# Reciprocal square roots as one power on GpSimd, weight splits on VectorE, last squares straight into the column sums

## The chip, the cores and the metric

The kernel runs on one core of one Trainium2 chip. The metric is the device time of one execution in microseconds (us), as the median of several runs. In the profile PE is TensorE (PEld its weight loads), DVE is VectorE, ACT is ScalarE, POOL is GpSimd and SP is SyncE, whose queue here issues the weight transfers. An L with a number is a line of the kernel; the changed kernel has fewer lines, so its numbers are a little smaller for the same statement.

## The reference

A sequence `x` of 256 tokens with 1024 features, and a context `ctx` of the same size, pass through two blocks in float32. The first block has two layers, each with a modulated feed-forward part, a convolution (layer 0) or windowed attention (layer 1), and a second feed-forward part; a norm with a learned gain closes it. The second block has two layers: a mixer (two kinds of block attention in layer 0, a compressed, a selected and a windowed attention in layer 1), a feed-forward part, and a gated embedding. What matters here is that a root mean square norm stands before every part, and over every head of 64 features of the second block's queries and keys:

```python
def rmsnorm(x, g):
    y = x * lax.rsqrt(jnp.mean(x * x, axis=-1, keepdims=True) + NORM_EPS)
    return y * g

def modulate(x, g, shift, scale):
    return rmsnorm(x, g) * (1 + scale) + shift

def swiglu(h, w_in, w_out):
    gate, up = jnp.split(h @ w_in, 2, axis=-1)
    return (jax.nn.silu(gate) * up) @ w_out

def first_block(...):
    for i in range(DEPTH):
        x = x + 0.5 * gt1 * swiglu(modulate(x, g1, sh1, sc1), ffn1_wi[i], ffn1_wo[i])
        ctx = ctx + 0.5 * cg1 * swiglu(modulate(ctx, g1, ch1, cs1), ffn1_wi[i], ffn1_wo[i])
        ...                              # convolution or attention on both, gated
        x = x + 0.5 * gt3 * swiglu(modulate(x, g3, sh3, sc3), ffn2_wi[i], ffn2_wo[i])
    return rmsnorm(x, final_g)

def second_block(...):
    for i in range(DEPTH):
        h = h + mixer(rms(h, norm_mix[i]))          # rms over each head of q and k inside
        h = h + swiglu(rms(h, norm_ffn[i]), ...)
        h = h + sigmoid(rms(h, norm_ple[i]) @ w_ple_gate[i]) * (p[i] @ w_ple_proj[i])
    return h
```

## The kernel before

Activations lie with features on the 128 partitions, in 8 chunks of 128 features by 256 tokens; the two sequences of the first block are called streams (0 is `x`, 1 is `ctx`). Every product of float32 matrices is made of three matmuls of a high and a low part (`mm3`, L337 to L339, and `mm_tm`, L360 to L362, for results with tokens on the partitions): high by high, high by low, low by high. So each weight tile that a DMA brings into a staging buffer `stg` is split: ACT copies it rounded into `wh` (L306), and a subtract makes `wl` (L308). That subtract runs on DVE, except that the first `on_pool[0]` of a tile's four or so pieces go to POOL. The number is `ABP` = 4, so all pieces, while the tiles of the first mixer of the second block are prepared, `NSP` = 2 for the second mixer, and 0 elsewhere; four pieces at the opening also go to POOL.

A norm works like this. As each chunk of the residual is finished (L657 in the feed-forward parts), `sq_add` squares it on ACT (L385) and POOL adds the square to an accumulator (L386). `rcol` sums over the features: `colsum` multiplies the accumulator with a column of ones on PE (L390), and DVE reads the result and adds epsilon (L397). `rsqrt_small` makes the reciprocal root with ten DVE instructions on 1 to 8 columns: a first guess by integer arithmetic (L370), then three Newton steps of three instructions (L373, L374, L376). `spread` turns the column into a row on all partitions: DVE scales the identity matrix with it (L406) and PE multiplies with ones (L407). In the first block `Mod.chunk` then modulates a chunk: DVE L543; for even chunks ACT L548 and DVE L549 give the high and low parts, for odd chunks ACT L551 and L552 and POOL L553 do. PE's first matmuls of the next part need these chunks, so each such seam of the first block is a chain from the last residual through PE, DVE and PE back to PE. In the second block, and for its first norm, `Norm` and `FinalNorm` let the matmuls start on unscaled activations and apply the root to their results. `FinalNorm.root` (L1373 to L1383) makes two roots one after the other, for the first block's closing norm and the second block's first; ACT's evictions of the projections (L1449) scale with the product of both.

In the mixers `qk_heads` calls `head_rms` for four heads on two token tiles: ACT squares (L1419), DVE scales epsilon (L1422), sums per head (L1423), takes the mean (L1425, two instructions), makes the root of 8 columns and applies it (L1437, two instructions); later PE transposes the result (L1463) and DVE moves it on (L1465). POOL also scales the rows of attention weights (L1485, L1486).

The program is emitted by loops over parts, layers and output tiles, with a small list of due times (`Flow`) that places side work between groups of matmuls; a scheduler of the framework then orders each engine's instructions. Engines run in that order and wait for each other by semaphores, so an instruction that waits holds up all that stands behind it on its engine. `look` asks for weights a tile or more ahead of their use. In the last rows below `L492` is DVE's sum that forms the modulation vectors.

## Time and profile before

| | |
|---|---|
| median of 3 runs | 2514.32 us (2513.06 to 2517.64) |
| the profiled execution | 2520.06 us, of which the trace spans 2518.2 |
| PE busy | 2360.3 us (94%) |
| DVE busy | 1754.9 us (70%), 3816 instructions |
| ACT busy | 1075.2 us (43%) |
| POOL busy | 569.3 us (23%), 595 instructions |
| the chain that ended last | PE 32%, DVE 9%, ACT 1% of the span (the page follows only a part of it) |
| granted clock of TensorE, mean | 0.97 |

A row of a timeline gives the start, the duration, the engine, the line and operation, the tiles written and read with their sizes, and how many instructions were put together; in brackets stands the idle time before it and what released it. A group of instructions gives the busy time of all, the mean of one, and the idle time before them with its releasers. A waiting PE counts twice: the pause itself, and the part of the work behind it at half clock, which the column of the granted clock shows (1.00 is 2.4 GHz, 0.5 is 1.2 GHz).

### The profile page before, as it was taken

To read this page: it belongs to the slowest core of one execution; us is meant where nothing else is said; L and a number is where in the kernel's file an instruction comes from. 1 tells how busy PE (TensorE), PEld (TensorE's weight loads), DVE (VectorE), ACT (ScalarE), POOL (GpSimd) and SP (SyncE) were. 2 spreads that over 40 slices of the span, in tenths; PEclk is the share of its full clock that TensorE was granted. 3 is DMA by queue.
4 is the path that set the end of the run, shared out by engine and by line. 5 is a ranking of instruction groups with operands and counts; after the bars stand their busy time and mean duration, and the time that the engine had idled before them with its cause. 6 is when DMAs were issued, how large, how long until landed. Compare 5 with 4: busy or idle time off the path is not lost. (4 is left out here: it accounts for less than half of the span.)

```text
span 2518.2 us, 40157 instructions
## 1 busy us (share of the span) xinstructions
PE 2360.3 (94%) x15397; PEld 2107.0 (84%) x15397; DVE 1754.9 (70%) x3816; ACT 1075.2 (43%) x2497; POOL 569.3 (23%) x595
## 2 busy tenths in 40 slices
PE   7999998766999999899999899999799999899999
PEld 5788887655888888888888888999699998879999
DVE  5567569887665745766546786767977678787667
ACT  3322223432532222332232485546455555665444
POOL 1100103665410010310010332104641112431101
PEclk9999998887999999999999999999899999999999
DMA  9745354152244535244546323865335556325553
GB/s 262 232 158 176 125 176 151 59 126 67 64 138 138 177 104 167 97 138 150 184 150 209 105 68 110 254 205 168 114 103 176 187 177 177 118 66 161 176 176 114
DMA packets 313149, 371.91 MB, mean 148 GB/s; under 512 B 9307, under 2 KB 298236, under 8 KB 305148
## 3 DMA queue, kind: packets, MB, share of 16 engines
q1 hardware_dynamic: 312380, 368.87, 46.1%
q8 instruction: 121, 1.98, 0.3%
q14 instruction: 72, 0.59, 0.1%
q10 hardware_dynamic: 576, 0.47, 0.1%
HBM read 364.06 MB, written 5.24 MB: 147 GB/s over the span
## 5 line engine op out<-in xcount | busy, mean ns | idle before, releaser
L337 PE MATMUL ps<-a,wh 128*128 128x256 f32 (+2 forms) x4032 | 1310.7, 327 | 20.3 <-ACT wh L306 9.2
L339 PE MATMUL ps<-a,wl 128*128 128x256 f32 (+2 forms) x4032 | 1310.0, 325 | 6.5 <-DVE wl L308 6.5
L338 PE MATMUL ps<-a,wh 128*128 128x256 f32 (+2 forms) x4032 | 1311.7, 326 | 3.7 <-DVE a L1290 1.4
L306 ACT ACTIVATE wh<-stg 128x512 fp32r<-128x512 f32 (+1 forms) x1280 | 609.5, 539 | 598.9 <-PE ps L338 328.5
L337 PEld LDWEIGHTS ps<-a,wh 128*128 128x128 f32 x4032 | 771.3, 192 | 93.1 <-ACT wh L306 11.2
L339 PEld LDWEIGHTS ps<-a,wl 128*128 128x128 f32 x4032 | 774.5, 192 | 68.0 <-DVE wl L308 7.5
L338 PEld LDWEIGHTS ps<-a,wh 128*128 128x128 f32 x4032 | 775.5, 192 | 66.6 <-POOL a L553 2.0
L308 DVE TENSOR_TENSOR wl<-stg,wh 128x512 fp32r<-128x512 f32 (+1 forms) x1206 | 692.7, 626 | 162.9 <-ACT wh L306 157.2
L561 POOL TENSOR_TENSOR a<-t,a 128x256 fp32r<-128x256 f32 (+1 forms) x128 | 136.2, 1066 | 1338.5 <-ACT a L560 1286.5
L492 DVE CUSTOM_DVE_ANT_0 void<-stg,cb,vec 128x1024 f32<-128x1024 f32 x208 | 276.7, 1330 | 41.3 <-DMA stg<-ada_t 37.4
L560 ACT ACTIVATE a<-t 128x256 fp32r<-128x256 f32 (+1 forms) x152 | 76.5, 504 | 254.9 <-DVE t L621 176.3
L657 DVE SCALAR_TENSOR_TENSOR a<-ps,mv,a 128x256 f32<-128x256 f32 x232 | 101.4, 477 | 77.2 <-PE ps L339 77.1
L621 DVE TENSOR_TENSOR t<-t,ps 128x512 f32<-128x512 f32 x66 | 45.4, 687 | 151.6 <-PE ps L339 139.1
L386 POOL TENSOR_TENSOR acc<-acc,t 128x256 f32<-128x256 f32 x98 | 95.7, 977 | 205.0 <-ACT t L385 201.8
L361 PE MATMUL ps<-wl,a 128*128 128x256 f32 x384 | 112.2, 292 | 8.2 <-DVE wl L308 6.9
L360 PE MATMUL ps<-wh,a 128*128 128x256 f32 x384 | 112.7, 294 | 1.7 <-ACT wh L306 1.7
L308 POOL TENSOR_TENSOR wl<-stg,wh 128x512 fp32r<-128x512 f32 (+1 forms) x74 | 93.8, 1296 | 88.7 <-ACT wh L306 88.7
L362 PE MATMUL ps<-wh,a 128*128 128x256 f32 x384 | 111.3, 290 | 0.0
L620 ACT ACTIVATE t<-ps 128x512 f32<-128x512 f32 x66 | 39.0, 590 | 108.2 <-PE ps L339 108.2
L361 PEld LDWEIGHTS ps<-wl,a 128*128 128x128 f32 x384 | 76.7, 200 | 9.7 <-DVE wl L308 7.3
L360 PEld LDWEIGHTS ps<-wh,a 128*128 128x128 f32 x384 | 76.5, 199 | 2.7 <-ACT wh L306 1.9
L841 DVE SCALAR_TENSOR_TENSOR a<-a,vec,a 128x512 f32<-128x512 f32 x76 | 78.3, 1095 | 0.0
(310 smaller groups left out, 1957.0 us busy)
## 6 DMA issues: line engine op xcount, KB each, us to landing
stg<-ffn_wi SPq DMA_DIRECT2D x86, 1024.0 KB, 5.1
stg<-ada_t SPq DMA_DIRECT2D x60, 1024.0 KB, 4.8
stg<-ffn_wo SPq DMA_DIRECT2D x48, 768.0 KB, 4.5
stg<-w_ffn_gate SPq DMA_DIRECT2D x22, 1024.0 KB, 5.4
stg<-w_ffn_up SPq DMA_DIRECT2D x22, 1024.0 KB, 5.7
stg<-w_ffn_down SPq DMA_DIRECT2D x24, 768.0 KB, 4.4
stg<-conv_pw_w SPq DMA_DIRECT2D x12, 1024.0 KB, 5.8
stg<-w_in_ab SPq DMA_DIRECT2D x12, 1024.0 KB, 5.1
```

Of the source, the lines that this page charges most:

```text
L306: nc.scalar.activation(wh[:, k], st[:, k], AF.Copy)
L308: e.tensor_tensor(wl[:, k], st[:, k], wh[:, k].bitcast(F32), ALU.subtract)
L337: nc.tensor.matmul(out, wh[:, k, js], h, start=(k == 0), stop=False)
L338: nc.tensor.matmul(out, wh[:, k, js], l, start=False, stop=False)
L339: nc.tensor.matmul(out, wl[:, k, js], h, start=False, stop=(k == n - 1))
L360: nc.tensor.matmul(out, h[:, ts], wh[:, k, :], start=(k == 0), stop=False)
L361: nc.tensor.matmul(out, h[:, ts], wl[:, k, :], start=False, stop=False)
L362: nc.tensor.matmul(out, l[:, ts], wh[:, k, :], start=False, stop=(k == n - 1))
L386: nc.gpsimd.tensor_tensor(acc, acc, t, ALU.add)
L492: nc.vector.tensor_tensor_reduce(self.void, st[:, i], self.cb[:, s], 1.0, V("ada_b", 72 * layer + v + i), ALU.mult, ALU.add, mv[layer][:, ...
L561: eng.tensor_tensor(l, src, h.bitcast(F32), ALU.subtract)
L657: nc.vector.scalar_tensor_tensor(x[s][:, m, :], o, g, x[s][:, m, :], ALU.mult, ALU.add)
```

## The change

Four edits. First, `rsqrt_small` is one POOL instruction, an elementwise power of the column with a constant tile of -0.5 (`mhalf`, written once at the start). Second, `on_pool` and its three numbers are gone, so weight splits run on DVE everywhere (the four at the opening stay on POOL). Third, the last square of a norm is no longer added to the accumulator; `colsum` multiplies both, the accumulator and the last square, with ones and lets PE add them up. Fourth, odd chunks are modulated as the even ones are, and in `head_rms` the scaled epsilon and the means are made on POOL instead of DVE, in front of the power.

```diff
+    mhalf = cp.tile([P, 16], F32, name="mhalf")
+    nc.vector.memset(mhalf, -0.5)
...
-            e = eng or (nc.gpsimd if i < share else nc.vector)
+            e = eng or nc.vector
             e.tensor_tensor(wl[:, k], st[:, k], wh[:, k].bitcast(F32), ALU.subtract)
...
     def rsqrt_small(v, out=None):
-        n = v.shape[1]
-        y = tiny()[:, :n]
-        nc.vector.tensor_scalar(y.bitcast(I32), v.bitcast(I32), -0.5, 1597463007.0, ALU.mult, ALU.add)
-        for i in range(3):
-            t = tiny()[:, :n]
-            nc.vector.scalar_tensor_tensor(t, y, -0.5, y, ALU.mult, ALU.mult)
-            nc.vector.tensor_tensor(t, t, v, ALU.mult)
-            z = out if (i == 2 and out is not None) else tiny()[:, :n]
-            nc.vector.scalar_tensor_tensor(z, t, 1.5, y, ALU.add, ALU.mult)
-            y = z
+        y = tiny()[:, :v.shape[1]] if out is None else out
+        nc.gpsimd.tensor_tensor(y, v, mhalf[:, :v.shape[1]], ALU.pow)
         return y
...
-    def colsum(p, c0, acc):
-        for t in range(acc.shape[1] // P):
-            nc.tensor.matmul(p[:, c0 + t:c0 + t + 1], acc[:, t * P:(t + 1) * P], ones[:, 0:1], start=True, stop=True)
+    def sq_last(src, scale=1.0):
+        t = tmp()[:, :S]
+        nc.scalar.activation(t, src, AF.Square, scale=scale)
+        return t
+    def colsum(p, c0, parts):
+        for t in range(parts[0].shape[1] // P):
+            for i, part in enumerate(parts):
+                nc.tensor.matmul(p[:, c0 + t:c0 + t + 1], part[:, t * P:(t + 1) * P], ones[:, 0:1],
+                                 start=(i == 0), stop=(i == len(parts) - 1))
...
-            sq_add(self.accs[s], x[s][:, m, :], m == 0)
+            if m < DC - 1:
+                sq_add(self.accs[s], x[s][:, m, :], m == 0)
+            else:
+                self.last[s] = sq_last(x[s][:, m, :])
...
-            if c % 2 == 0:
-                nc.scalar.activation(h, t, AF.Identity, bias=sh)
-                nc.vector.scalar_tensor_tensor(l, t, sh, h.bitcast(F32), ALU.add, ALU.subtract)
-            else:
-                nc.scalar.activation(t, t, AF.Identity, bias=sh)
-                nc.scalar.activation(h, t, AF.Copy)
-                nc.gpsimd.tensor_tensor(l, t, h.bitcast(F32), ALU.subtract)
+            nc.scalar.activation(h, t, AF.Identity, bias=sh)
+            nc.vector.scalar_tensor_tensor(l, t, sh, h.bitcast(F32), ALU.add, ALU.subtract)
...
-        nc.vector.tensor_scalar(e[:, 0:2], var, EPS, None, ALU.mult)
+        nc.gpsimd.tensor_scalar(e[:, 0:2], var, EPS, 0.0, ALU.mult, ALU.add)
         nc.vector.tensor_reduce(v, sq.rearrange("p (n d) -> p n d", d=64), AX.X, ALU.add)
         for t in range(2):
-            nc.vector.tensor_scalar(v[:, t * ng:(t + 1) * ng], v[:, t * ng:(t + 1) * ng], 1.0 / HD, e[:, t:t + 1],
+            nc.gpsimd.tensor_scalar(v[:, t * ng:(t + 1) * ng], v[:, t * ng:(t + 1) * ng], 1.0 / HD, e[:, t:t + 1],
                                     ALU.mult, ALU.add)
```

`Norm` and `FinalNorm` get the same edit of the last square as `Mod`. The scheduler orders the instructions anew, and three places of the new order matter below. The first is DVE at the start of the second block's first mixer, behind `FinalNorm.root`. Before, DVE goes through the first heads' norm and its root (the three Newton instructions at the end stand three times):

```order
L1422 TENSOR_SCALAR tn<-col 128x2
L1423 TENSOR_REDUCE tn<-t_15310 128x8
L1383 TENSOR_TENSOR col<-col,tn 128x2
L1425 TENSOR_SCALAR tn<-tn 128x4 x2
L370 TENSOR_SCALAR tn<-tn 128x8
L373 SCALAR_TENSOR_TENSOR tn<-tn 128x8
L374 TENSOR_TENSOR tn<-tn 128x8
L376 SCALAR_TENSOR_TENSOR tn<-tn 128x8
```

After (L1422 is now the sum per head, L1436 the scaling of the heads, L304 a weight split), the sum of one group of heads, the scaling, and the next group's sum follow with splits in between:

```order
L1422 TENSOR_REDUCE tn<-t_15073 128x8
L1382 TENSOR_TENSOR col<-col,tn 128x2
L304 TENSOR_TENSOR wl<-stg,wh 128x512
L1436 TENSOR_TENSOR t_15072<-t_14919,tn 128x256 x2
L304 TENSOR_TENSOR wl<-stg,wh 128x512
L1422 TENSOR_REDUCE tn<-t_15086 128x8
L304 TENSOR_TENSOR wl<-stg,wh 128x512
L1436 TENSOR_TENSOR t_15085<-t_14920,tn 128x256 x2
L304 TENSOR_TENSOR wl<-stg,wh 128x512 x6
L1422 TENSOR_REDUCE tn<-t_15228 128x8
L304 TENSOR_TENSOR wl<-stg,wh 128x512
L1436 TENSOR_TENSOR t_15227<-t_15162,tn 128x256 x2
```

What moved: the roots and means have left DVE, and weight splits stand between the heads' steps, two ahead of the second group's scaling and seven ahead of the third's.

The second is POOL at the same place. Before, it adds the last squares (L386) and then has 26 splits in a row, then scales rows of attention weights:

```order
L308 TENSOR_TENSOR wl<-stg,wh 128x512 x2
L386 TENSOR_TENSOR t_14901<-t_14901,t_15117 128x256
L386 TENSOR_TENSOR t_14901<-t_14901,t_15120 128x256
L308 TENSOR_TENSOR wl<-stg,wh 128x512 x26
L1485 TENSOR_SCALAR a_15739<-a_15739,tn 128x128
L1486 TENSOR_SCALAR a_15739<-a_15739,tn 128x256
```

After, the adds (L375) are followed by the two powers of `FinalNorm.root` and the means and powers of the heads, three rows for each `head_rms`:

```order
L375 TENSOR_TENSOR t_14692<-t_14692,t_14881 128x256
L375 TENSOR_TENSOR t_14692<-t_14692,t_14884 128x256
L366 TENSOR_TENSOR col<-tn,mhalf 128x2
L366 TENSOR_TENSOR tn<-tn,mhalf 128x2
L1421 TENSOR_SCALAR tn<-col 128x2
L1424 TENSOR_SCALAR tn<-tn 128x4 x2
L366 TENSOR_TENSOR tn<-tn,mhalf 128x8
```

What moved: the splits are gone, and POOL's part of each norm stands in their place.

The third is DVE at the second-stream seam in front of the convolution, where stream 1's root is made. Before, sums for the modulation vectors (L492, listed in two rows each) stand between the reading of the column sums (L397) and the first steps of the root; two more such sums and the rest of the steps follow before the scaled identity for the broadcast (L406):

```order
L397 TENSOR_SCALAR col<-ps 128x2
L492 ISA void,mv_89<-stg,cb,vec 128x1024
L492 ISA mv_89 128x1
L370 TENSOR_SCALAR tn<-col 128x2
L492 ISA void,mv_89<-stg,cb,vec 128x1024
L492 ISA mv_89 128x1
L373 SCALAR_TENSOR_TENSOR tn<-tn 128x2
```

After, one such sum (L489) stands between the reading (L394) and the scaled identity (L403), while POOL makes the power:

```order
L394 TENSOR_SCALAR col<-ps 128x2
L489 ISA void,mv_91<-stg,cb,vec 128x1024
L489 ISA mv_91 128x1
L403 TENSOR_SCALAR t_3267<-ident,col 128x128 x2
L489 ISA void,mv_91<-stg,cb,vec 128x1024
L489 ISA mv_91 128x1
```

What moved: ten root instructions have left, and three of the four long sums no longer stand in front of the broadcast.

## Rows read from the trace of the kernel before

**Rows 1.** Head of the page: span, then busy time of each engine.
```profile
span 2518.2 us, 40157 instructions
PE 2360.3 (94%) x15397; PEld 2107.0 (84%) x15397; DVE 1754.9 (70%) x3816; ACT 1075.2 (43%) x2497; POOL 569.3 (23%) x595
```

**Rows 2.** PE's waits: engine, line, releaser: us, times, longest us.
```profile
PE ps L907 <- DMA a<-gated: 22.3, 2, 21.8
PE ps L407 <- DVE t L406: 19.0, 9, 5.2
PE ps L1463 <- DVE t L1437: 18.3, 3, 16.3
PE ps L390 <- POOL acc L386: 9.7, 5, 3.1
PE ps L361 <- DVE wl L308: 6.9, 2, 3.8
```

**Rows 3.** Timeline of PE: start us, us, operation, idle before and releaser.
```profile
1794.40 0.47 PE L1463 MATMUL ps<-ident,t 128*128 128x128 f32 x1 [16.33 <-DVE t L1437]
```

**Rows 4.** Timeline of DVE over the same stretch.
```profile
1755.26 1.22 DVE L373 SCALAR_TENSOR_TENSOR tn<-tn 128x2 f32<-128x2 f32 x1
1765.22 0.16 DVE L373 SCALAR_TENSOR_TENSOR tn<-tn 128x2 f32<-128x2 f32 x1
1793.92 0.76 DVE L1437 TENSOR_TENSOR t<-t,tn 128x256 f32<-128x256 f32 x2
```

**Rows 5.** Timeline of POOL and ACT over the same stretch.
```profile
1753.91 10.06 POOL L308 TENSOR_TENSOR wl<-stg,wh 128x512 fp32r<-128x512 f32 x8 [0.69 <-ACT wh L306]
1772.16 0.64 ACT L1419 ACTIVATE t<-t 128x512 f32<-128x512 f32 x1
```

**Rows 6.** Stretches: us; busy PE, PEld, DVE, ACT, POOL; clock; DMA.
```profile
1753.00:1800.00 47.00, 30.67 (x236) 30.11 (x235) 43.03 (x94) 18.55 (x40) 30.55 (x25) 0.82 0.49 157
1800.00:1860.00 60.00, 54.82 (x457) 50.74 (x456) 49.61 (x150) 35.69 (x101) 35.19 (x44) 0.97 0.27 89
2120.00:2240.00 120.00, 98.99 (x744) 92.25 (x743) 98.03 (x347) 74.05 (x212) 48.19 (x69) 0.91 0.25 80
```

**Rows 7.** Groups of DVE by line: busy us, mean ns, idle before.
```profile
L373 DVE SCALAR_TENSOR_TENSOR tn<-tn 128x2 f32<-128x2 f32 (+3 forms) x102 | 32.1, 315 | 2.8
L376 DVE SCALAR_TENSOR_TENSOR tn<-tn 128x8 f32<-128x8 f32 (+3 forms) x87 | 26.8, 308 | 2.6
L374 DVE TENSOR_TENSOR tn<-tn 128x8 f32<-128x8 f32 (+3 forms) x54 | 20.1, 372 | 1.6
L549 DVE SCALAR_TENSOR_TENSOR a<-t,mv,a 128x256 fp32r<-128x256 f32 x40 | 20.2, 513 | 1.2 <-ACT a L548 1.2
L492 DVE CUSTOM_DVE_ANT_0 void<-stg,cb,vec 128x1024 f32<-128x1024 f32 x208 | 276.7, 1330 | 41.3 <-DMA stg<-ada_t 37.4
```

**Rows 8.** Groups of POOL and DVE by form, columns as before.
```profile
L308 POOL TENSOR_TENSOR wl<-stg,wh 128x512 fp32r<-128x512 f32 x72 | 93.0, 1319 | 87.3 <-ACT wh L306 87.3
L1485 POOL TENSOR_SCALAR a<-a,tn 128x128 f32<-128x128 f32 x32 | 11.9, 372 | 47.8 <-DVE tn L1523 26.2 <-DVE tn L1859 17.1 <-ACT a L1144 2.9
L1836 POOL MEMSET a<- 128x64 f32 x4 | 0.6, 149 | 10.5 <-PE ps L1904 10.5
L308 DVE TENSOR_TENSOR wl<-stg,wh 128x512 fp32r<-128x512 f32 x724 | 502.8, 743 | 120.2 <-ACT wh L306 115.3 <-issue 0.8 <-PE ps L338 0.2
```

**Rows 9.** Timelines of POOL and PE at a second-stream seam.
```profile
679.19 1.18 POOL L386 TENSOR_TENSOR acc<-acc,t 128x256 f32<-128x256 f32 x1 [0.88 <-ACT t L385]
680.42 1.01 PE L390 MATMUL ps<-ones,acc 128*128 128x1 f32 x4 [3.05 <-POOL acc L386]
```

**Rows 10.** Timelines of DVE and PE at two other seams.
```profile
427.88 0.15 DVE L397 TENSOR_SCALAR col<-ps 128x2 f32<-128x2 f32 x1
434.92 0.71 PE L407 MATMUL ps<-t,ones 128*128 128x128 f32 x4 [1.61 <-DVE t L406]
1432.97 1.19 PE L407 MATMUL ps<-t,ones 128*128 128x128 f32 x4 [5.20 <-DVE t L406]
```

More of the change, by code (lines that the diff above doesn't have):

```diff
@@ L42 @@
 PIVN = 1
-GQP = 0
-ABP = 4
-NSP = 2
 CTX3 = 4.0
@@ L287, in wtile @@
         return w
-    on_pool = [0]
     def weight(src, kc, cols, pool=None, eng=None):
@@ L386, in sq_add, with rcol @@
             nc.gpsimd.tensor_tensor(acc, acc, t, ALU.add)
-    def colsum(p, c0, acc):
-        for t in range(acc.shape[1] // P):
-            nc.tensor.matmul(p[:, c0 + t:c0 + t + 1], acc[:, t * P:(t + 1) * P], ones[:, 0:1], start=True, stop=True)
-    def rcol(acc):
-        n = acc.shape[1] // P
+    def sq_last(src, scale=1.0):
[7 more added lines that the diff above has]
+                                 start=(i == 0), stop=(i == len(parts) - 1))
+    def rcol(parts):
+        n = parts[0].shape[1] // P
         p = bank()
-        colsum(p, 0, acc)
+        colsum(p, 0, parts)
         v = np_.tile([P, 4], F32, name="col", bufs=6)[:, :n]
@@ L518, in __init__ @@
             self.layer, self.j, self.streams = layer, j, streams
-            self.accs, self.cols, self.acts = {}, {}, {}
+            self.accs, self.last, self.cols, self.acts = {}, {}, {}, {}
         def set_acts(self, acts):
@@ L528, in add @@
                 self.accs[s] = np_.tile([P, S], F32, name="acc", bufs=2)
-            sq_add(self.accs[s], x[s][:, m, :], m == 0)
+            if m < DC - 1:
+                sq_add(self.accs[s], x[s][:, m, :], m == 0)
+            else:
+                self.last[s] = sq_last(x[s][:, m, :])
         def rc(self, s):
-            _, self.cols[s] = rcol(self.accs[s])
+            _, self.cols[s] = rcol([self.accs[s], self.last[s]])
         def ap(self, s):
@@ L1294, in add @@
                 nc.vector.tensor_tensor(l[:, S:], sh, h[:, S:].bitcast(F32), ALU.subtract)
-            sq_add(self.acc, src, c == 0)
+            if c < DC - 1:
+                sq_add(self.acc, src, c == 0)
+            else:
+                self.last = sq_last(src)
         def root(self):
-            self.var, self.col = rcol(self.acc)
+            self.var, self.col = rcol([self.acc, self.last])
         def wide(self):
@@ L1313, in tile_kernel @@
     out_proj(a["attn_w_o"][0], wo_evac)
-    on_pool[0] = 0
     W = 384
@@ L1363, in add @@
             nc.vector.scalar_tensor_tensor(l, xs, g, h.bitcast(F32), ALU.mult, ALU.subtract)
-            sq_add(self.acc[:, 0], xs, c == 0)
-            sq_add(self.acc[:, 1], xs, c == 0, V("final_g", c))
+            if c < DC - 1:
+                sq_add(self.acc[:, 0], xs, c == 0)
+                sq_add(self.acc[:, 1], xs, c == 0, V("final_g", c))
+            else:
+                self.last = [sq_last(xs), sq_last(xs, V("final_g", c))]
         def root(self):
             p = bank()
-            colsum(p, 0, self.acc[:, 0])
-            colsum(p, 2, self.acc[:, 1])
+            for i in range(2):
+                colsum(p, 2 * i, [self.acc[:, i], self.last[i]])
             st = tiny()
@@ L1497, in causal_pv @@
         flow.adv(0.33)
-    on_pool[0] = ABP
     qT = slot([P, DC, S])
@@ L1651, in mlp_and_ple @@
         ple(layer, npl, nxt, pacts, then)
-    on_pool[0] = 0
     nf = res_norm("norm_ffn", 0)
@@ L1930, in tile_kernel @@
             queries_nsa(NS_ORDER[:i].count("q"))
-    on_pool[0] = 0
     nf = res_norm("norm_ffn", 1)
```

3 lines of the change are left out of this document (removed).

## The prediction

> **What bounds the kernel now.** I read the page's head first: PE is busy 2360.3 of 2518.2 us, 94% [rows 1]. So the change can win only PE's idle time, some 158 us, and the half-clock work behind each pause; saved DVE or POOL time counts only where it ends a PE wait. The next view is therefore PE's waits by releaser [rows 2]. The reader is to see two kinds there. The longest (L907 on gated DMAs, 22.3 us) is untouched by the diff. The others shown are its own: L407, the broadcast of a norm's root, waits 19.0 us in 9 places; L1463, the transposed heads of the second block, 18.3 us, of which one wait is 16.3; L390, the column sums, 9.7 us in 5; L361, a projection that waits for its low weights, 6.9 us in 2. That is 53.9 us of waits that the change can reach.
>
> Third, the timeline at the longest of these. PE stops at 1778.07 and starts again at 1794.40 [rows 3]: it waits for DVE's L1437, the end of a chain of Newton steps. A step on two columns takes 0.16 us when DVE is alone (the one that starts at 1765.22, [rows 4]), one per 0.2 us, and 1.22 us while POOL runs a weight split (start 1755.26); POOL runs eight splits without a pause from 1753.91 for 10.06 us [rows 5]. So a root of ten steps, 2 us alone, takes several times that here. The stretch table says the same: 43.03 of 47 us on DVE are busy from 1753 to 1800, and PE has 30.67, at a granted clock of 0.82, a mean of parts at 2.4 and parts at 1.2 GHz [rows 6].
>
> **The change part by part.** One root falls from 10 DVE instructions to one POOL instruction, 34 times. By the groups [rows 7] the steps of L373 (32.1 us), L376 (26.8) and L374 (20.1) alone are 79.0 us of DVE time. DVE receives 70 splits, on which POOL spent 1319 ns and it spends 743 [rows 8], 52 us, and 40 low parts of odd chunks at 513 ns [rows 7], 20.5. By these rows DVE's balance is even or better, all of it beside PE, and I give it no price of its own.
>
> *The power itself.* No row shows a power on POOL. The nearest from below is a memset of 128x64, 149 ns; an arithmetic operation with a scalar on 128x128 takes 372 ns; a subtract of two operands on 128x512, 1319 ns [rows 8]. The power has 1 to 8 columns but more work in each. I take 0.8 us, between the last two and below the split, keep 0.15 and 1.5 us as ends, and treat more than that as a rival, since no row here computes a function. A small POOL operation (L1421, L1424 after) I take at 0.25 us, between the memset and the scalar operation, and 0.2 us for each passage between engines (the spacing of DVE's steps).
>
> *Start of the second block's mixer (1753 to 1800).* The three pieces of order show what happens: the splits leave POOL, and DVE has them between the heads' steps. The new chain begins at 1754.7, when DVE has read the sums (the first step of [rows 4] is the fifth instruction after that): the root's small steps 0.4 and 0.6; the first heads 0.8 (POOL) and 0.8 (L1436 twice; a pair is 0.76, [rows 4]); the second heads' sum 0.7, two splits 1.2, POOL 0.5, L1436 0.8; before the third seven splits 4.2 (about 0.6 each where POOL runs none; at 743 ns it would be 1 us more), the sum 0.7, POOL 0.5, L1436 0.8; five passages 1.0. These are 13 us, so 1767.7 plus five powers: 1771.7 at 0.8 us. The third heads' squares are there at 1772.80 [rows 5], and sum, POOL, power, L1436 and passages after them take 3.4, so they are ready at 1776.2, ahead of 1778.07. The whole wait of 16.33 us goes, up to a power of (1778.7 - 1767.7)/5 = 2.2 us. The work behind the pause runs at half clock; I take 0.7 for that, as some of it may stay behind the next wait. Sum 17. What is late next is PE itself.
>
> *The rest of that mixer (1800 to 1860).* PE has 54.82 of 60 us [rows 6]; its pauses come mostly from the same blocked steps. I take 3.5 of the 5.2 us.
>
> *Column sums.* The last square reaches PE without POOL's add. At 679.19 that add takes 1.18 us, and L390 starts as it ends, after an idle 3.05 us [rows 9]. The five waits of 9.7 us [rows 2] lose 1.1 each, 5.5. Against it, each of 14 sums needs as many matmuls again, four records, 0.4 us at full clock (1.01 us at half, [rows 9]): 5.6 us, and 0.8 for the last norm of the first block. Half of the seams had the time idle anyway, but I charge it all.
>
> *The roots of the norms.* In the first block PE has matmuls of its own between the column sums and the broadcast. At the seam of rows 10 DVE reads the sums at 427.88, PE works on until 433.31 (434.92 less its wait of 1.61), so a chain under 5.4 us costs nothing; before it is longer, since DVE's order puts a sum for modulation vectors (1330 ns, [rows 7]) between the first steps, four times (third piece of order). After, one such sum stands there: 0.2 for the read, 1.3 for the sum with the power beside it, 0.6 for the scaled identity. That is about 2, or 1.2 + p for a power p above 1.1 us, and the wait is gone for any p below some 4 us. In the first-stream seams residual adds and splits stand there, 2 to 8 of them at some 0.5 us, about what was mixed into the steps before; their waits go likewise, with the steps. At the seam after the attention the rope work mostly stays in front, so of the 5.20 us [rows 10] only 1.3 goes; the opening and the convolution's root have little beside them: ten steps of 0.2 us become 0.8 and a passage, so each keeps some 0.9. Of the nine waits [rows 2] these two seams have 1.61 and 5.20 us and the other seven 12.2; 1.6 + 1.3 + (12.2 - 1.8) = 13.3 goes. Shorter pauses give perhaps 1 us of clock back.
>
> *Odd chunks.* Two ACT steps and one POOL subtract become one ACT and one DVE step, as the even ones are. DVE then has two operations a chunk, about 1 us, beside PE's twelve matmuls of it, and the chunk's POOL step is gone, so the cost is nothing; if DVE were late by a step, each of ten groups would cost 0.5.
>
> *The later mixer (2120 to 2240).* PE is busy 98.99 of 120 us, DVE 98.03 [rows 6]. L361's 6.9 us are there. The 22 splits that POOL did are 16 us more on DVE, the steps and their blocking about as much less. But POOL's scale operations (372 ns and more) and memsets now stand ahead of powers. I take 7 us, with 0 and 14 as ends. Everywhere else (the feed-forward seams) PE works through the roots: nothing.
>
> **Sum:** 17 + 3.5 + 5.5 - 6.4 + 13.3 + 1 + 7 = 40.9. The profiled execution took 2520.06 us, 1.9 more than its span, and the median of the runs is 2514.32, so 5.7 lower. 2520.06 - 40.9 = 2479.2 for an execution like that one, 2473.4 on the median: I say 2474.
>
> **Two rules beside it.** A step of DVE that reads two operands waits for POOL here (1.22 against 0.16 us, [rows 4]). The Trainium skill, "SBUF — State Buffer", section "Who interferes with whom", says that such an instruction contends with a GpSimd instruction that reads SBUF; the trace agrees with those numbers. It speaks against the change too, since a power reads two operands beside DVE's splits: if each of a dozen powers on the path waited for one split of 743 ns, the sum would be about 32. The other rule stands in rival two.
>
> **The rivals.**
> 1. *DVE becomes the bound in the mixers.* For it: 43.03 of 47 and 98.03 of 120 us busy now [rows 6], and all splits join. Against it: the stretch of 47 us has 25 of POOL's splits at most, 19 us, and loses more than that in blocked steps. If the splits came late, the first mixer would gain half and the later one lose 6: 40.9 - 9 - 13 = 19, or 2495.
> 2. *A power is dear, and the kernel is slower.* If it costs p us, the first mixer's chain pays five times what is over 2.2, some six other chains in the mixers pay it over 1.5, and eight seams over 4.3. 40.9 - 5 (p - 2.2) - 6 (p - 1.5) - 8 (p - 4.3) is 0 at p = 5, the point from which it decides; at 7 us it is 40.9 - 24 - 33 - 21.6 = -38, or 2552. For it: POOL is the dearer engine for the split, 1319 against 743 ns, and a power is no single step. Against it: small POOL operations take 149 and 372 ns [rows 8]. The Trainium skill, "GPSIMD Engine Reference", section 2.1, gives about 6 us for the first call of freshly loaded code on this engine: paid once, at the opening, the sum would be about 35; paid each time that POOL changes from adds to powers, it would be this rival. No run here shows it.
> 3. *The wait is only exchanged.* Powers between 1.5 and 5 us, or queued behind POOL's adds and scale operations: by the same formula 3.5 us leaves 40.9 - 6.5 - 12 = 22, or 2492. For it: POOL's adds before the sums and its scale operations stay, in front of powers. Against it: POOL loses 93.0 us of splits [rows 8].
>
> **How the numbers follow.** Forecast 63%, rival one 13%, rival two 10%, rival three 14%. The forecast's own spread comes from the ends: a power of 0.15 us, 14 us in the later mixer and the 1.7 us left in the first give some 53 of gain, 2461; none in the later mixer, half of the clock and the rest, 28, or 2486. The range takes in rivals one and three: 2460 to 2506. A measurement can tell 0.2%, 5 us, from no change: faster means below 2509. The forecast and nearly all of rivals one and three lie there, 0.85; their edges and those of rival two around no change 0.06; slower 0.09.
>
> **What would show it.** In the profile after: the wait of 16.3 us before the heads' transposes (L1462 there) is gone and that stretch's clock near 1; L366 on POOL has a mean below 1.5 us; the column sums wait below 1 us each; the broadcasts wait about 6 us in all, most of it after the attention; DVE's splits rise to some 1276 and POOL keeps four. A mean above 2.2 us, or PE waiting on DVE's splits for more than 10 us in the mixers, makes the prediction wrong.

## The result, and the profile after

The changed kernel takes 2478.1 us (median of 4 runs, 2477.74 to 2482.5) against 2513.69 for the kernel before (4 runs): a ratio of 0.986, 95% interval 0.9843 to 0.9877. That is 35.6 us less. The prediction was 2474, within 2460 to 2506.

The busy times of the changed kernel (its span is 2476.0 us), which answer to [rows 1]:

```profile
PE 2348.9 (95%) x15461; PEld 2100.2 (85%) x15461; DVE 1692.7 (68%) x3545; ACT 1064.1 (43%) x2457; POOL 488.8 (20%) x545
```

PE has lost 11 us of busy time although it has 64 more matmuls, so part of the gain is clock: the mean granted clock is 0.979 where it was 0.970. PE's waits by line and releaser (total us, times, longest) answer to [rows 2]; L902 is the convolution's long wait (L907 before, 22.3 us), L404 the broadcast, L386 the column sums, L1494 a matmul behind transposed rows, L357 a projection that waits for low weights:

```profile
PE ps L902 <- ACT t L849: 24.7, 1, 24.7
PE ps L404 <- DVE t L403: 9.6, 7, 3.3
PE ps L386 <- POOL acc L375: 7.3, 4, 2.5
PE ps L1494 <- DVE a L1140: 6.6, 2, 5.3
PE ps L357 <- DVE wl L304: 5.3, 2, 3.5
```

The wait for the heads' transposes, 18.3 us before, no longer stands among them. The broadcasts fell from 19.0 to 9.6 us, the column sums from 9.7 to 7.3, the low weights from 6.9 to 5.3. New is L1494 with 6.6 us.

The power itself, by form (busy us, mean ns, idle before):

```profile
L366 POOL TENSOR_TENSOR tn<-tn,mhalf 128x8 f32<-128x8 f32 x14 | 23.0, 1640 | 1.2
L366 POOL TENSOR_TENSOR col<-col,mhalf 128x2 f32<-128x2 f32 x14 | 12.9, 924 | 61.1 <-DVE col L394 61.1
L366 POOL TENSOR_TENSOR tn<-tn,mhalf 128x4 f32<-128x4 f32 x1 | 1.0, 1018 | 14.8 <-DVE tn L699 14.8
```

So a power takes 0.70 us on 2 columns, 1.02 on 4 and 1.64 on 8: about 0.4 us and 0.155 a column. The group of 14 at the norms has a mean of 924 ns: ten of them take 0.70 or 0.71 us, one 0.87, and three 1.67 to 1.69; those three start inside one of DVE's sums for the modulation vectors (L489, 1.27 us).

The start of the second block's first mixer, POOL and then DVE, answers to [rows 4, 5]:

```profile
1731.99 0.70 POOL L366 TENSOR_TENSOR tn<-tn,mhalf 128x2 f32<-128x2 f32 x1 [0.67 <-DVE tn L1379]
1733.08 0.93 POOL L1424 TENSOR_SCALAR tn<-tn 128x4 f32<-128x4 f32 x2
1734.09 1.64 POOL L366 TENSOR_TENSOR tn<-tn,mhalf 128x8 f32<-128x8 f32 x1
1735.77 0.76 DVE L1436 TENSOR_TENSOR t<-t,tn 128x256 f32<-128x256 f32 x2 [2.26 <-POOL tn L366]
```

Power, two means and power follow each other on POOL, and L1436, where DVE applies the root, starts 0.04 us after the power ends. Three stretches of the changed kernel (columns as in [rows 6]) show the first seam of the first block, the start of the mixer, and what follows it:

```profile
395.00:427.00 32.00, 25.53 (x204) 24.32 (x202) 31.05 (x61) 11.28 (x26) 12.62 (x15) 1.00 0.40 132
1729.00:1764.00 35.00, 33.16 (x279) 32.45 (x279) 25.14 (x64) 20.28 (x46) 12.77 (x18) 1.00 0.54 169
1764.00:1800.00 36.00, 30.66 (x245) 27.80 (x246) 21.61 (x61) 19.73 (x59) 13.80 (x25) 0.91 0.31 99
```

From 1729 to 1764 PE has 33.16 of 35 us at a clock of 1.00, where before a comparable stretch had 30.67 of 47 at 0.82. In the next 36 us it has only 30.66.

### Where the time went, by stage

The last column-sum matmul of a norm is a mark that all kernels have. The table gives the us between such marks in one profiled execution each: the first block up to the sum of its closing norm; the first mixer up to the next norm's sum; the feed-forward part and embedding; the second mixer; the rest of the span. The rows below the second are the experiments of the next section.

| kernel | first block | first mixer | between | second mixer | rest | median of runs |
|---|---|---|---|---|---|---|
| before | 1754.4 | 138.3 | 228.2 | 174.8 | 222.5 | 2513.7 to 2515.4 |
| changed | 1729.4 | 125.1 | 229.0 | 171.4 | 221.1 | 2478.1 |
| splits_only | 1750.2 | 120.6 | 228.0 | 165.6 | 221.5 | 2487.1 |
| power_only | 1724.7 | 131.2 | 227.9 | 172.8 | 220.7 | 2480.5 |
| splits_back | 1729.6 | 138.6 | 228.7 | 178.0 | 221.3 | 2500.5 |
| heads_newton | 1729.0 | 114.2 | 228.6 | 161.5 | 221.5 | 2458.4 |
| means_on_dve | 1730.8 | 120.3 | 228.7 | 166.9 | 221.1 | 2470.2 |
| newton_splits_back | 1735.9 | 134.8 | 228.6 | 171.1 | 221.1 | 2488.0 |
| power_twice | 1738.8 | 141.9 | 228.8 | 181.7 | 221.0 | 2510.1 |
| squares_back | 1732.0 | 125.5 | 227.8 | 172.6 | 221.2 | 2476.4 |
| chunks_back | 1726.0 | 126.0 | 228.9 | 171.9 | 221.1 | 2473.7 |
| newton_and_chunks | 1724.3 | 114.1 | 228.6 | 160.7 | 221.0 | 2453.8 |
| power_and_splits | 1730.7 | 113.9 | 227.7 | 159.9 | 220.8 | 2455.0 |

The first column is to be read with care: splits_only changes next to nothing in the first block, and yet it stands 4.2 us below the kernel before. One execution's first block varies by about that, 3 us of it ahead of the first mark. A further cause is known: in four of the profiles (before, splits_only, squares_back, power_twice) a single add of POOL in the convolution takes 9.96 or 9.97 us instead of 1.18 or 1.19. Here it is in the kernel before and in the changed one, each with what DVE does beside it:

```profile
527.37 9.96 POOL L951 TENSOR_TENSOR acc<-t,t 128x256 f32<-128x256 f32 x1
527.40 9.35 DVE L841 SCALAR_TENSOR_TENSOR a<-a,vec,a 128x512 f32<-128x512 f32 x14
```

```profile
516.41 1.18 POOL L946 TENSOR_TENSOR acc<-t,t 128x256 f32<-128x256 f32 x1
516.92 0.74 DVE L819 SCALAR_TENSOR_TENSOR t<-ps,vec,t 128x512 f32<-128x512 f32 x1
```

In the four long cases the add starts 0.02 or 0.03 us ahead of 14 operations of DVE that read two operands from SBUF and follow each other without a pause, and it ends 0.6 us after the last of them. In the nine others it starts 0.5 us ahead of L819, the operation in front of that run, and is over when the run begins. The difference is made one instruction before: POOL's copy, released by a DMA's landing, starts 0.62 to 0.69 us ahead of the same DVE operation (L824, L819 after) in the four and 1.26 to 1.56 us ahead in the nine. In these 13 traces an add that has missed its place waits for the whole run.

PE's wait behind these adds is 14.1 to 15.2 us in the four profiles and 10.9 to 11.6 in the nine; the stretch from the second seam's broadcast to the convolution's takes 175.7 to 176.5 us in the four and 171.2 to 172.8 in eight others (174.8 in newton_splits_back). Whether it goes with the execution or with the kernel is not shown, as each kernel has one profile: the profiled executions of squares_back and power_twice are the longest of their kernels' runs (2480.89 and 2514.03 us), but that of splits_only is not (2487.64 of 2485.41 to 2488.16). If it goes with the execution, then of the 25.0 us that the first block shows, about 8 belong to the executions and 17 to the change, by estimate. With 13.2 and 3.4 for the mixers and 0.6 for the rest this makes 34, and the medians say 35.6.

### The profile page after: what moved, and what is told of

Its sections match the earlier page's. It is cut to its first block, busy times and chain, and to the rows that moved or that the text cites. A ratio compares the mean times of both kernels' runs of the same rounds, so it can differ in the third digit from the quotient of the medians.

```text
span 2476.0 us, 39874 instructions
## 1 busy us (share of the span) xinstructions
PE 2348.9 (95%) x15461; PEld 2100.2 (85%) x15461; DVE 1692.7 (68%) x3545; ACT 1064.1 (43%) x2457; POOL 488.8 (20%) x545
## 5 line engine op out<-in xcount | busy, mean ns | idle before, releaser
L304 DVE TENSOR_TENSOR wl<-stg,wh 128x512 fp32r<-128x512 f32 (+1 forms) x1276 | 729.3, 624 | 163.8 <-ACT wh L302 159.3
L489 DVE CUSTOM_DVE_ANT_0 void<-stg,cb,vec 128x1024 f32<-128x1024 f32 x208 | 273.6, 1316 | 41.2 <-DMA stg<-ada_t 37.4
L375 POOL TENSOR_TENSOR acc<-acc,t 128x256 f32<-128x256 f32 x84 | 82.3, 980 | 211.6 <-ACT t L374 208.8
L357 PE MATMUL ps<-wl,a 128*128 128x256 f32 x384 | 110.5, 288 | 5.3 <-DVE wl L304 5.3
L836 DVE SCALAR_TENSOR_TENSOR a<-a,vec,a 128x512 f32<-128x512 f32 x76 | 88.0, 1223 | 0.0
L357 PEld LDWEIGHTS ps<-wl,a 128*128 128x128 f32 x384 | 75.5, 196 | 5.9 <-DVE wl L304 5.9
L356 PEld LDWEIGHTS ps<-wh,a 128*128 128x128 f32 x384 | 75.5, 197 | 2.8 <-ACT wh L302 1.9
L358 PEld LDWEIGHTS ps<-wh,a 128*128 128x128 f32 x384 | 75.4, 196 | 0.0
```

Of the source, the lines that this page charges most:

```text
L304: e.tensor_tensor(wl[:, k], st[:, k], wh[:, k].bitcast(F32), ALU.subtract)
L356: nc.tensor.matmul(out, h[:, ts], wh[:, k, :], start=(k == 0), stop=False)
L357: nc.tensor.matmul(out, h[:, ts], wl[:, k, :], start=False, stop=False)
L358: nc.tensor.matmul(out, l[:, ts], wh[:, k, :], start=False, stop=(k == n - 1))
L489: nc.vector.tensor_tensor_reduce(self.void, st[:, i], self.cb[:, s], 1.0, V("ada_b", 72 * layer + v + i), ALU.mult, ALU.add, mv[layer][:, ...
L836: nc.vector.scalar_tensor_tensor(y, src, wk, y, ALU.mult, ALU.add)
```

## The experiments

All times are medians of 4 to 10 runs beside runs of the kernel before on the same chip. Ratios stand against that kernel. Each kernel has line numbers of its own, a few more or less for the same statement; where two fences follow each other, the first is named first.

### The splits alone

```diff
 # kernel before
-ABP = 4
-NSP = 2
+ABP = 0
+NSP = 0
```

> The kernel before with all weight splits on DVE and nothing else changed (the ten-step roots stay on DVE). Theory one, that the steps were slow because POOL's splits blocked them: at the start of the second block's mixer each step falls to about 0.2 us, the wait of 16.3 us before the heads' transposes falls to under 3, and the median to about 2495. Theory two, that the chain is long by its number of steps: the wait keeps 8 us or more and the median is 2505 or above.

Measured: 2487.08 us, ratio 0.9886 (0.987 to 0.9903). A group of DVE's Newton steps on 8 columns (busy us, mean ns) in the kernel before and in splits_only, and two of PE's waits in the latter:

```profile
L373 DVE SCALAR_TENSOR_TENSOR tn<-tn 128x8 f32<-128x8 f32 x42 | 13.5, 322 | 1.3
```

```profile
L373 DVE SCALAR_TENSOR_TENSOR tn<-tn 128x8 f32<-128x8 f32 x42 | 7.3, 173 | 0.9
```

```profile
PE ps L407 <- DVE t L406: 18.3, 9, 5.2
PE ps L1463 <- DVE t L1437: 6.5, 2, 4.8
```

Those steps had a mean of 322 ns before and have 173 now, and the wait before the heads' transposes fell from 18.3 to 6.5 us, the broadcasts' hardly from 19.0. The mixers became 17.7 and 9.2 us shorter (table). Theory one holds, and the time fell by more than expected, 28 us without any power, although the longest wait kept 4.8 us where under 3 was expected.

### The power alone

```diff
 # kernel before; splits, chunks, squares and the heads' means stay
     def rsqrt_small(v, out=None):
-        ...                                  # ten DVE instructions
+        y = tiny()[:, :v.shape[1]] if out is None else out
+        nc.gpsimd.tensor_tensor(y, v, mhalf[:, :v.shape[1]], ALU.pow)
```

> The kernel before with the power on POOL and nothing else changed (splits, odd chunks, last squares and the heads' means as before). Theory one: at the first block's seams the broadcasts' waits of 19.0 us fall to about 8, but in the first mixer the powers queue behind POOL's splits of 1.3 us, so the wait of 16.3 us stays between 10 and 20; median 2498 to 2508. Theory two, that the power itself brings the mixer's gain: that wait falls below 5 us and the median is 2490 or less.

Measured: 2480.5 us, ratio 0.9863 (0.9843 to 0.9882). PE's waits for broadcasts (L402), for the heads' transposes (L1458) and for DVE's copies L1141 in the first mixer, and from DVE's waits that to apply the heads' roots (L1432):

```profile
PE ps L402 <- DVE t L401: 4.2, 4, 1.3
PE ps L1458 <- DVE t L1432: 3.0, 2, 1.9
PE ps L1490 <- DVE a L1141: 5.8, 1, 5.8
```

```profile
DVE t L1432 <- POOL tn L372: 35.4, 14, 5.3
```

Theory one failed: the time is below what theory two named, and the wait of 16.3 us fell below 5, as theory two had it. But the mixers gave 7.1 and 2.0 us only, since other waits came in its place (5.8 us at L1490), and the first block nearly 30, of which some 22 are left by the estimate that takes off 8 for the executions. The broadcasts' waits fell to 4.2 us. I had expected queueing behind splits to eat the gain; it did cost, as DVE waits 35.4 us for powers, but the steps on 8 columns that they replaced had taken 47.9 us. Splits alone and power alone, 28 and 35 us, do not add up to the change: in the mixers both remove the same wait.

### Splits back on POOL, with the rest of the change

```diff
 # changed kernel
-            e = eng or nc.vector
+            e = eng or (nc.gpsimd if i < share else nc.vector)      # share 4, 2 in the mixers
```

> The changed kernel with the splits of the two mixers back on POOL (4 and 2 pieces of a tile). Theory one, powers and means queue behind POOL's splits and DVE's steps are blocked by them: 2490 to 2505, with the long wait at the start of the first mixer back at 8 us or more. The rival, that freeing DVE of 70 splits helps it now that the roots are gone: 2478 or less.

Measured: 2500.5 us, ratio 0.9941 (0.9922 to 0.9961), 22 us above the changed kernel. Three of PE's waits (L1500 and L1524 follow DVE's copies and scalings in the first mixer, L363 a POOL split, nearly all of it in the second):

```profile
PE ps L1500 <- DVE a L1146: 8.9, 2, 7.3
PE ps L1524 <- DVE a L1470: 8.0, 1, 8.0
PE ps L363 <- POOL wl L310: 6.1, 6, 4.3
```

Theory one's time came, though not as one long wait at the start: the waits are spread, with 8.9, 8.0 and 6.1 us in these rows. Against power_only, which has the same splits and powers, it loses 7.4 and 5.2 us in the mixers. The main difference there is that the heads' means are on POOL too, behind splits; that this is the cause was not tried by itself.

### The heads' roots back on DVE

```diff
 # changed kernel, head_rms only
-        nc.gpsimd.tensor_scalar(e[:, 0:2], var, EPS, 0.0, ALU.mult, ALU.add)
+        nc.vector.tensor_scalar(e[:, 0:2], var, EPS, None, ALU.mult)
...
-            nc.gpsimd.tensor_scalar(v[:, t * ng:(t + 1) * ng], ...
+            nc.vector.tensor_scalar(v[:, t * ng:(t + 1) * ng], ...
-        r = rsqrt_small(v)
+        r = rsqrt_newton(v)                      # the ten DVE instructions of before
```

> The changed kernel with the heads' means and roots (8 columns, 14 of them) made by DVE in ten steps again; the 2-column roots stay powers on POOL. Theory one, that the later part of the first mixer and the second mixer lost because DVE stands still while POOL makes means and a power of 1.64 us, behind POOL's scaling of attention weights: the waits of 5.3 us and 3.5 us after 1774 and 2107 us shrink by half or more and the median is 2470 to 2475. The rival, that ten steps cost DVE as much as the wait: 2478 to 2484.

Measured: 2458.36 us, ratio 0.9778 (0.9763 to 0.9793): 19.7 us below the changed kernel, where 3 to 8 were expected. What DVE and POOL do in the changed kernel at the new wait shows why:

```profile
1771.47 0.65 DVE L1422 TENSOR_REDUCE tn<-t 128x8 f32<-128x512 f32 x1
1772.04 0.68 DVE L304 TENSOR_TENSOR wl<-stg,wh 128x512 fp32r<-128x512 f32 x1
1776.37 0.42 DVE L1436 TENSOR_TENSOR t<-t,tn 128x256 f32<-128x256 f32 x1 [3.65 <-POOL tn L366]
1777.11 1.98 DVE L304 TENSOR_TENSOR wl<-stg,wh 128x512 fp32r<-128x512 f32 x3
1779.01 1.47 DVE L1140 COPY a<-ps 128x384 f32<-128x384 f32 x3
1773.98 0.64 POOL L1424 TENSOR_SCALAR tn<-tn 128x4 f32<-128x4 f32 x2
1774.70 1.64 POOL L366 TENSOR_TENSOR tn<-tn,mhalf 128x8 f32<-128x8 f32 x1
1779.70 0.70 PE L1494 MATMUL ps<-a,a 128*64 128x256 f32 x2 [5.34 <-DVE a L1140]
```

The heads' sums are ready at 1772.12. POOL first finishes scaling attention weights, makes two means (0.64 us) and the power (1.64). DVE has one split to do and then stands idle for 3.65 us with L1436 at its head. Behind L1436 stand three splits and the copies L1140, and PE's L1494 waits 5.34 us for the first of those. The group of L1436 gives the sum over all 14 heads' norms (last column: idle before it):

```profile
L1436 DVE TENSOR_TENSOR t<-t,tn 128x256 f32<-128x256 f32 (+1 forms) x28 | 12.0, 458 | 37.6 <-POOL tn L366 37.6
```

DVE stands still for 37.6 us there. In heads_newton PE's wait for the heads' transposes (L1475) is small, and the same group of DVE (L1449) waits for next to nothing:

```profile
PE ps L1475 <- DVE t L1449: 2.7, 2, 1.7
```

```profile
L1449 DVE TENSOR_TENSOR t<-t,tn 128x256 f32<-128x256 f32 (+1 forms) x28 | 11.7, 457 | 0.2
```

Ten steps of 0.17 to 0.2 us keep DVE busy for 2 us; means, power and queue on POOL keep it idle for 1.8 to 4.7 at 13 of the 14 places. The mixers take 114.2 and 161.5 us instead of 125.1 and 171.4, which is the whole 20 us. Theory one is confirmed by the wait that it names.

### Only the means back on DVE

```diff
 # changed kernel, head_rms only: the two edits of nc.gpsimd.tensor_scalar above, with r = rsqrt_small(v)
```

> The changed kernel with the heads' scaled epsilon and means on DVE again and the power on POOL. By POOL's rows each such group stands 0.9 us (three operations) before the power, on DVE 0.4: with 14 groups, some half of them on the way to PE, 2474 to 2477. The rival, that POOL's queue ahead of the power decides: within 1 us of 2478.

Measured: 2470.24 us, ratio 0.9824 (0.9807 to 0.984): 7.9 us below the changed kernel, again more than the 1 to 4 expected, 4.8 in the first mixer and 4.5 in the second. So of the 20 us some 8 are the means and some 12 the power of 8 columns with its queue.

### Heads' roots on DVE, splits on POOL

```diff
 # heads_newton, with the edit of splits_back
```

> The changed kernel with the heads' means and roots on DVE and the mixers' splits back on POOL (4 and 2 pieces). Theory one, that DVE's small steps of two operands stand still while POOL splits: the heads' steps take 0.3 us and more in the mean and the median is 2472 to 2482, 14 to 24 above heads_newton. The rival, that the place of the heads' roots alone decided: within 4 us of heads_newton's 2458.

Measured: 2488.01 us, ratio 0.9889 (0.9872 to 0.9906), 29.7 above heads_newton and more than expected. A step's group, and PE's wait for the heads' transposes (L1481 here):

```profile
L381 DVE SCALAR_TENSOR_TENSOR tn<-tn 128x8 f32<-128x8 f32 x42 | 16.6, 396 | 1.3
```

```profile
PE ps L1481 <- DVE t L1455: 15.2, 4, 13.4
```

The steps are back at 396 ns and the long wait is back at 13.4 us. With splits on DVE a step on 8 columns has 173 ns, with splits on POOL 322 to 396: the blocked steps are shown by the edit that makes them and the edit that ends them. The four kernels form a square:

| | splits on POOL | splits on DVE |
|---|---|---|
| heads' means and roots on POOL | 2500.5 | 2478.1 |
| heads' means and roots on DVE | 2488.0 | 2458.4 |

Each row gains by moving the splits (22.4 and 29.6), each column loses by moving the heads' roots to POOL (12.5 and 19.7).

### Every power twice

```diff
 # changed kernel
         nc.gpsimd.tensor_tensor(y, v, mhalf[:, :v.shape[1]], ALU.pow)
+        nc.gpsimd.tensor_tensor(y, v, mhalf[:, :v.shape[1]], ALU.pow)
```

> The changed kernel with every power made twice in a row into the same place, 34 powers more: +0.7 to 0.9 us for 2 columns and +1.64 for 8. If the seams hide it, as the prediction said for a power up to 4 us, and the heads' chains in the two mixers pay it, the median is 2484 to 2492 and the growth lies all behind 1730 us. The rival, that it is hidden everywhere: 2480 or less; that it is paid everywhere: 34 powers or 45 us, above 2505.

Measured: 2510.14 us (10 runs), ratio 0.9983 (0.9974 to 0.9993): 32 us more, beyond the 2484 to 2492 expected and within what the rival "paid everywhere" named. The stages say where it is paid. PE's wait for broadcasts:

```profile
PE ps L405 <- DVE t L404: 12.3, 6, 4.1
```

The mixers grew by 16.8 and 10.3 us, 27.1 in all, where 14 more powers of 1.64 us are 23.0 and the two roots of the closing norm 1.4: there the power is paid in full, and a little more. The first block grew by 9.4, of which 5.2 is the convolution's stretch with its long POOL add; the broadcasts' waits grew by 2.7 only. So the seams do hide most of a power, as the prediction had it, and the heads none of it; the expectation failed in what it put on the heads.

### The last squares back

```diff
 # changed kernel, the same in Norm and FinalNorm
-            if m < DC - 1:
-                sq_add(self.accs[s], x[s][:, m, :], m == 0)
-            else:
-                self.last[s] = sq_last(x[s][:, m, :])
+            sq_add(self.accs[s], x[s][:, m, :], m == 0)
```

> The changed kernel with the last squares added by POOL again and single column sums. By the prediction's terms (5.5 us won, 6.4 us of matmuls paid) the median stays within 3 us of 2478, with PE about 6 us less busy and the waits before the column sums some 5 us longer. The rival, that the shorter chain gave most of what the seams won: 2485 or above.

Measured: 2476.38 us (2471.64 to 2480.89), ratio 0.9844 (0.9822 to 0.9865). Busy times, and PE's wait for the column sums:

```profile
PE 2346.1 (95%) x15397; PEld 2096.6 (85%) x15397; DVE 1689.1 (68%) x3545; ACT 1063.9 (43%) x2457; POOL 506.3 (20%) x561
```

```profile
PE ps L386 <- POOL acc L375: 11.3, 5, 3.3
```

PE is 2.8 us less busy and waits 4.0 us longer. The median is 1.7 us below the changed kernel's, within the spread of its own runs: no effect that can be told. Neither rival's 2485 nor a gain.

### The odd chunks back

```diff
 # changed kernel, Mod.chunk
+            if c % 2 == 0:
                 nc.scalar.activation(h, t, AF.Identity, bias=sh)
                 nc.vector.scalar_tensor_tensor(l, t, sh, h.bitcast(F32), ALU.add, ALU.subtract)
+            else:
+                nc.scalar.activation(t, t, AF.Identity, bias=sh)
+                nc.scalar.activation(h, t, AF.Copy)
+                nc.gpsimd.tensor_tensor(l, t, h.bitcast(F32), ALU.subtract)
```

> The changed kernel with odd chunks modulated by two ACT steps and one POOL subtract again. The prediction gave this edit no price. Theory one: PE's first matmuls behind a broadcast wait about 3 us more in all over the seams, 2481. The rival, no effect: within 1.5 us of 2478.

Measured: 2473.74 us, ratio 0.9838 (0.9823 to 0.9852): 4.4 us faster than the changed kernel, against both expectations. The waits for broadcasts:

```profile
PE ps L404 <- DVE t L403: 6.1, 6, 1.8
```

The broadcasts wait 3.5 us less. At the second-stream seam in front of the attention PE's wait for the broadcast is 1.28 us, and 3.25 in the changed kernel. DVE's order there differs; first the changed kernel, then chunks_back:

```profile
1407.24 1.71 DVE L1107 TENSOR_TENSOR a<-t,t 64x256 f32<-64x256 f32 x4
1408.99 0.48 DVE L403 TENSOR_SCALAR t<-ident,col 128x128 f32<-128x128 f32 x2
```

```profile
1406.22 0.28 DVE L403 TENSOR_SCALAR t<-ident,col 128x128 f32<-128x128 f32 x1
1406.42 1.71 DVE L1112 TENSOR_TENSOR a<-t,t 64x256 f32<-64x256 f32 x4
```

The root itself had been ready in the changed kernel since 1402.82: the scheduler has put four adds of the rope in front of the scaled identity. At another seam POOL's add in front of the column sums is late, beside four splits of DVE, in all seven kernels that have the new odd chunks and in none of the six others:

```profile
1028.56 3.06 POOL L375 TENSOR_TENSOR acc<-acc,t 128x256 f32<-128x256 f32 x1
1028.55 2.48 DVE L304 TENSOR_TENSOR wl<-stg,wh 128x512 fp32r<-128x512 f32 x4
1032.47 0.38 PE L386 MATMUL ps<-ones,acc 128*128 128x1 f32 x2 [2.33 <-POOL acc L375]
```

It ends 0.6 us after DVE's run, like the long add above. From the sums before to these sums the changed kernel takes 17.6 us and chunks_back 15.9. So part of the price is the order and the neighbours that the edit brings about, and not DVE's added work as such; what the other seams pay was not separated. That the edit costs is shown twice, here and in the next experiment.

### What is left when the costly edits are undone

```diff
 # newton_and_chunks: heads_newton with the edit of chunks_back
 # power_and_splits: newton_and_chunks with the edit of squares_back
```

> The changed kernel with two of its edits undone: the heads' means and roots on DVE in ten steps, and odd chunks by two ACT steps and POOL. If the two add up, 2478.1 less 19.7 and 4.4: 2454, and the best of all so far. The rival, that with the heads' means gone from POOL the odd chunks' place no longer matters: 2458 to 2460.

> As newton_and_chunks, and the last squares added by POOL again: what is left of the change is the power for the norms' roots of 2 columns and the splits on DVE. Theory one, that the last squares' matmuls cost PE about what the shorter chain wins: within 3 us of newton_and_chunks, and 30 us below splits_only, which differs from it by the norms' powers alone. The rival, that the last squares matter once nothing else waits: 5 us or more above newton_and_chunks.

Measured: newton_and_chunks 2453.78 us (5 runs), ratio 0.9761 (0.9748 to 0.9775); power_and_splits 2454.95 us (4 runs), ratio 0.9762 (0.9748 to 0.9776). The two undone edits add up as expected, 2454. The last squares again make no difference. power_and_splits differs from splits_only by the norms' powers alone, 20 instructions, and stands 32.1 us below it, as theory one said. By the stages 12.4 us of that lie in the mixers and the most in the first block, where up to 4 or 5 may be the long POOL add, which the profile of splits_only has. The best kernel of this study is thus 60 us faster than the one before and 24 faster than the changed one: it keeps the norms' powers and the splits on DVE, and gives the heads' roots and the odd chunks back.

## Why the prediction was right, and where not

The time and its sign were right, 2478.1 against 2474 and inside the range, and the largest single mechanism was the one named. But the terms were off in both directions, and that the sum came within 5 us is in part luck.

*The power.* 0.8 us was taken; 2 columns measured 0.70 alone and 0.92 in the mean. 8 columns took 1.64, above the upper end of 1.5, because one value was used for all sizes. Nothing is paid on top at a change of operation, the condition for rival two's second reading: each of the heads' 14 powers starts 0.08 us behind the mean in front of it on POOL. The Trainium skill, "GPSIMD Engine Reference", section 2.1, has about 6 us for a first call of freshly loaded code; nothing of the kind shows at the first power of the kernel, which starts 0.08 us after its operand is ready and takes 1.02 us on 4 columns, like the others in proportion.

*Start of the first mixer, 17 us.* Right in kind and size. From the closing norm's sum to the broadcast that follows in the mixer, at 1806 us before and at 1764 after, the changed kernel gained 17.0 us (its lead grew from 25.0 to 42.0), the wait is gone and the clock of 1729 to 1764 is 1.00. PE's idle time in that stretch fell from 16.3 to 1.5 us; the other 2.2 us are clock, where 0.7 was allowed for it. The mechanism, POOL's splits blocking DVE's steps, is shown by splits_only and newton_splits_back. The Trainium skill, "SBUF — State Buffer", section "Who interferes with whom", says that a DVE instruction with two SBUF inputs contends with a GpSimd instruction that reads SBUF. These runs agree: a step of two operands falls from 322 to 173 ns when POOL no longer splits.

*The rest of that mixer, +3.5 us.* This step failed: it lost 3.8 (the stage's 13.2 less 17.0). The prediction watched whether the heads' roots were ready before PE wanted them at the start, and found slack of 2.2 us a power (2.1 by its own 1778.07 us, as it divides with 1778.7). It did not ask the same at the later heads, where POOL has attention weights to scale in front and DVE's queue has copies that PE waits for behind L1436. Rival three named the queue ("queued behind POOL's adds and scale operations") with 14%, and it came true there, for that part alone.

*The second mixer, 7 us.* 3.4: the same step. One wait of PE for a split that stands behind L1436 has 3.49 us; DVE and PE in the changed kernel:

```profile
2108.95 1.29 DVE L1436 TENSOR_TENSOR t<-t,tn 128x512 f32<-128x512 f32 x2 [2.54 <-POOL tn L366]
2110.17 2.49 DVE L304 TENSOR_TENSOR wl<-stg,wh 128x512 fp32r<-128x512 f32 x4
2110.91 0.58 PE L357 MATMUL ps<-wl,a 128*128 128x256 f32 x1 [3.49 <-DVE wl L304]
```

heads_newton gets 13.3 there, close to the upper end that was given.

*Column sums, 5.5 won and 6.4 paid.* The waits lost 2.4 instead of 5.5; at one seam it is an add that DVE's splits hold up (1028.56 above), at the others the cause stays open. PE was charged 6.4 and squares_back shows 2.8. The net is near zero in both accounts.

*Roots of the norms, 13.3 us.* The waits lost 9.4. The seam that the prediction places after the attention (the wait of 5.20 us) is the second stream's in front of it; the rope's adds do stay in front of the broadcast there, as it said, and 3.25 us of that wait are left, where 3.9 were reckoned. At the seam of [rows 10], where the whole 1.61 us were to go, 1.54 stay: the chain from DVE's read of the sums to the scaled identity fell from 6.7 to 1.95 us, as forecast, but the read itself comes 3.6 us after the sums (at 423.33, behind splits and modulation sums of DVE), where it came 0.4 us after them before. By the estimate above the first block as a whole gained about 17 where the terms gave 13.4, the opening's with them, although the odd chunks took 4.4 of it; power_only, without the new chunks, has some 22. So the norms' roots were under-sized. Part of that is clock, put at 1 us. At the first seam the row before is

```profile
399.00:436.00 37.00, 27.10 (x185) 25.91 (x183) 35.97 (x80) 11.66 (x28) 17.71 (x18) 0.86 0.44 142
```

and the clock is 1.00 now (395 to 427 above). At the next three seams it is about as before (0.90, 0.94 and 0.89, now 0.88, 0.93 and 0.91), so the clock alone is not shown to be the whole difference. The 32 us between splits_only and power_and_splits, a few less without the long add, say that the norms' powers are the most valuable part of the change.

*Odd chunks, nothing.* The step failed by 4.4 us. The prediction set the chunk's work beside PE's twelve matmuls of it, and found room; what it did not ask is what the new order puts in front of the broadcast, and which POOL add then meets a run of splits.

*The signs.* Of those named, the long wait is gone, and the powers' mean stays below 1.5 us (1.19 over all 34). DVE has 1280 splits and POOL four. But the column sums wait up to 2.5 us and not below 1, and the broadcasts 9.6 us and not about 6. Rival one, DVE as the bound in the mixers, did not come: PE waits 5.3 us for splits there.

The two misses in the mixers, some 11 us together, and that of the first block in the other direction, partly cancelled; this is the luck in the sum.

## What to carry to other kernels

An engine that works in order pays for a result made elsewhere with all its idle time up to that result, and hands this on to all that stands behind the waiting instruction; ten short steps of one's own can be cheaper than one instruction of a neighbour. Ask this of every place where a helper is called, not of the one that shows the longest wait: the powers won some 30 us at the norms, where DVE waits 9.9 us in all for 20 of them, and with the means lost 20 at the heads, where it waits 37.6 us for 14. And two edits that remove the same wait are not worth their sum. Last, a moved instruction changes its neighbours: look at what the new order puts in front of a waiting instruction and beside an operation of the other engine, before the moved work itself is blamed.

## What the runs showed of the hardware

A power of POOL costs 0.70 us on 128x2, 1.02 on 128x4 and 1.64 on 128x8, linear with some 0.155 us a column. DVE operations on a few columns take 0.17 us alone and up to 1.2 us while POOL subtracts two operands of 128x512; that holds for tensor_scalar steps with one SBUF input too, whose 14 of 8 columns had 360 ns before and 175 in splits_only. It goes the other way too: a POOL add of two operands of 128x256 took 1.18 us at one place in 9 of 13 profiles and 9.96 in 4, where it started just as DVE began 14 operations with two SBUF operands without a pause (9.35 us); another took 3.06 us beside four splits of DVE (2.48 us). Both end 0.6 us after DVE's run. So where one DVE step waits for the one POOL operation beside it, a POOL operation here waited for a whole run of DVE's.
